# Layer 1's modulation written into PSUM banks, and two feature tiles of the first token half between the halves of V

## The chip, the cores and the metric

The kernel runs on one core of a Trainium2 chip. The time is the device time in microseconds (us) of one execution of the whole program. Beside the timed runs there is one profiled execution, whose trace the rows below come from.

TensorE is called PE in the profile (PEld is its weight load), VectorE is DVE, ScalarE is ACT, GpSimd is POOL, and SP issues DMAs.

## The reference, cut to what matters

Two layers of an encoder over 1024 tokens of width 1024. Each layer normalises its input, scales and shifts it by columns that depend on the conditioning vector (the modulation), projects it, attends, and adds the result back. The change lies at the seam: the end of layer 0, the modulation of layer 1 and the first projections of layer 1.

```python
h = rms_norm(x, norm_w[layer]) * (1.0 + scale[:, None, :]) + shift[:, None, :]
...
proj = h @ w_in
qc, kc, vc, gc = jnp.split(proj, [C_Q, C_Q + C_KV, C_Q + 2 * C_KV], axis=-1)
oc = windowed_sink_attention(qc.reshape(b, s, C_KV_HEADS, C_GROUPS, HEAD_DIM),
...
return (oc * jax.nn.silu(gc)) @ w_out
```

## The kernel before

Activations are kept transposed: 128 features on the partitions, tokens along the free dimension. The 1024 tokens are worked in two halves of 512, the 1024 features in eight tiles of 128 (KC = 8). Each float32 factor is split into a high part and a low remainder, so that one product costs three matmuls (mm3): high by high, high by low, low by high. So the modulated input of layer 1 exists as hT10h, hT10l (first token half) and hT11h, hT11l (second half).

No instruction is issued where it stands in the code. A Recorder collects every operation with its operands; `run` (line 249) lays them out in time by a list of cost estimates, and `emit` (line 477) issues them in that order, so that each engine executes a fixed order. Among the operations whose operands are ready and whose buffers are free, an engine takes the one with the lowest number: the number is the place in the program, plus a shift where one is given. FILL_SHIFT = 150 (line 44) puts the projections that fill gaps 150 places behind. PSUM has eight banks; PA (line 543) takes one, which comes free after the last operation on it. The estimate also keeps a VectorE instruction with two tensor inputs in SBUF and a GpSimd instruction from running at one time (`held`, line 450). All instructions are issued from line 483, so that every row says L483 and tells by its tile names what it is.

The stage that the change touches, in program order:

- layer0_out (line 1470), once for each token half: the output projection of layer 0 (eight feature tiles of 24 matmuls), the residual sum into `xr`, the sum of squares, and rstd_rows (line 678), which leaves the reciprocal norm of every token, spread over all partitions, in one PSUM bank. rows_copy (line 707) copies this bank to SBUF as `rby`. Then modulate (line 712) runs for each of the eight feature tiles: VectorE multiplies `xr` by the scale column and by `rby`, in place; ScalarE adds the shift and rounds to the high part h; VectorE adds the shift again and subtracts h, which gives the low part.
- V (line 1507): for each of eight token tiles of 128, 24 matmuls of 256 columns with the modulated input as weights, then a ScalarE and a VectorE instruction that bring the high and low part to SBUF. Tiles 0 to 3 need the first token half, 4 to 7 the second.
- Feature tiles of K, Q and the gate (fts, line 1663 on): each has two halves, one for each token half, of 24 matmuls of 512 columns. `fill` (line 1669) takes the next of them off the list `halves`, with the shift of 150. Six are placed ahead of the windowed attention: k0 for both halves, q0 for both, q1 for both. The weights of a tile are loaded by SP and split by GpSimd (high) and GpSimd again (low); wk1f0 is that of k0, wq1f0 that of q0.
- The windowed attention (win_S, win_PV), with the other 30 halves between its blocks.

A mark on a load, as marks["op", 0, 1, 6], makes the plan issue it no sooner than the start of that matmul (output projection of layer 0, second half, feature tile 6).

Of the kernel before, what the change touches and what calls it, by code (L numbers as in the profile page):

```python
# [14 lines left out]
ALU = mybir.AluOpType  # L15
# [7 lines left out]
NT = T // P  # L23
# [26 lines left out]
LAT_SHIFT = 100  # L50
FILL_J = (0,)
K2_POOL = 1
MOD_WAY = (("dve",), ("dve",))
E_START = (4, 4)
WARM = (32, 14, 20)
SQ_ENG = ("dve", "pool", "pool")
# [449 lines left out]
def encoder_kernel(ctx: ExitStack, tc: tile.TileContext, xt, ada_t, w_c1, w_c2, w_c3, w_g0, w_uq, w_ukv, w_out0, w_v1,  # L506
                   w_f1, w_out1, cols_d, rows_d, tabs_d, out, dump=None):
    if dump is None:
# [7 lines left out]
    psum = psp.tile([P, 4096], F32, name="psum")  # L516
# [7 lines left out]
    nc = rec = Recorder(tc.nc, tc, psum, {"u": U_BUFS, "ua": UA_BUFS, "sm": SM_BUFS}, window=WINDOW,  # L524
                        reserve=RESERVE)
    mm = nc.tensor.matmul

    def U(name, dt=F32):
        return rec.tile(up, [P, 1024], dt, name, "u")

    def UR(name):
        return U(name, F32R)
# [4 lines left out]
    def SM(name):  # L537
        return rec.tile(smp, [P, 16], F32, name, "sm")
# [4 lines left out]
    def PA(name):  # L543
        return rec.bank(1, name)
# [11 lines left out]
    @contextmanager  # L556
    def issue_after(mark):
        before = rec.after_now
        rec.after_now = mark if mark is not None else before
        yield  # L560
        rec.after_now = before
# [5 lines left out]
    def f(ap):  # L567
        return ap.bitcast(F32)
# [4 lines left out]
    def sub(o, a, b):  # L573
        nc.vector.tensor_tensor(out=o, in0=a, in1=b, op=ALU.subtract)
# [14 lines left out]
    def transposes(outs, ins, last):  # L589
# [3 lines left out]
        for j in order:  # L593
            with issue_after(m_):
                t_ = nc.tensor.transpose(out=outs(j), in_=ins[j], identity=ident)
            if last is not None:
# [11 lines left out]
                                   op0=ALU.add, op1=ALU.mult)  # L608
    cb = U("cb")
    for j in range(2):  # L610
        pt = PT(f"cb{j}")
        for k in range(4):
# [7 lines left out]
                                   op0=ALU.add, op1=ALU.mult)  # L620
# [5 lines left out]
    def warm(n, mark):  # L626
        pt = PT(f"warm{mark.i}")
        with rec.at(shift=5000), issue_after(mark):
            for _ in range(n):
                nc.tensor.transpose(out=pt[:, 0:P], in_=ident, identity=ident)  # L630
# [31 lines left out]
    def A_col(l, kc):  # L662
        return mods[:, 16 * l + 2 * kc:16 * l + 2 * kc + 1]

    def sh_col(l, kc):
        return mods[:, 16 * l + 2 * kc + 1:16 * l + 2 * kc + 2]


    def add_squares(acc, src, first, name, eng):

        if first:
            nc.scalar.activation(acc, src, AF.Square)
            return
        t = U(name)[:, 0:src.shape[1]]
        nc.scalar.activation(t, src, AF.Square)
        eng.tensor_tensor(out=acc, in0=acc, in1=t, op=ALU.add)

    def rstd_rows(accs, name):

        n = accs[0].shape[1]  # L680
        nt = n // P
        v = None
        for k, acc in enumerate(accs):
            pt = PA(f"st{name}")
            for j in range(nt):
                m_ = nc.tensor.transpose(out=pt[:, j * P:(j + 1) * P], in_=acc[:, j * P:(j + 1) * P], identity=ident)
            ss = SM("ss")
            nc.vector.tensor_reduce(out=ss[:, 0:nt], in_=pt[:, 0:n].rearrange("p (t c) -> p t c", t=nt), axis=AX.X,
                                    op=ALU.add)
            if k == 0:  # L690
                nc.vector.tensor_scalar(ss[:, 4:4 + nt], ss[:, 0:nt], 1.0 / D, EPS, op0=ALU.mult, op1=ALU.add)
            else:
                nc.vector.scalar_tensor_tensor(out=ss[:, 4:4 + nt], in0=ss[:, 0:nt], scalar=1.0 / D, in1=v, op0=ALU.mult,
                                               op1=ALU.add)
            v = ss[:, 4:4 + nt]
        if name == "x0" and WARM[1]:
            warm(WARM[1], m_)
        r = SM("r")
        nc.gpsimd.tensor_tensor(out=r[:, 0:nt], in0=v, in1=mhalf[:, 0:nt], op=ALU.pow)
        pr = PA(f"rb{name}")  # L700
        for j in range(nt):
            m_ = nc.tensor.transpose(out=pr[:, j * P:(j + 1) * P], in_=r[:, j:j + 1].broadcast_to([P, P]), identity=ident)
        if name == "x0" and WARM[2]:
            warm(WARM[2], m_)
        return pr[:, 0:n]

    def rows_copy(pr, name):
        rb = U(f"rb{name}")[:, 0:pr.proto().shape[1]]
        nc.scalar.copy(rb, pr)
        return rb  # L710

    def modulate(l, kc, src, rb, hl, way):

        h, lo = hl
        if way == "normed":
            nc.scalar.activation(h, src, AF.Identity, bias=sh_col(l, kc), scale=A_col(l, kc))
            nc.scalar.activation(src, src, AF.Identity, bias=sh_col(l, kc), scale=A_col(l, kc))
            sub(lo, src, f(h))
        elif way == "pool":
            nc.gpsimd.tensor_tensor(out=src, in0=src, in1=rb, op=ALU.mult)  # L720
            nc.scalar.activation(h, src, AF.Identity, bias=sh_col(l, kc), scale=A_col(l, kc))
            nc.gpsimd.tensor_scalar(src, src, A_col(l, kc), sh_col(l, kc), op0=ALU.mult, op1=ALU.add)
            sub(lo, src, f(h))
        else:
            nc.vector.scalar_tensor_tensor(out=src, in0=src, scalar=A_col(l, kc), in1=rb, op0=ALU.mult, op1=ALU.mult)
            nc.scalar.activation(h, src, AF.Identity, bias=sh_col(l, kc))
            nc.vector.scalar_tensor_tensor(out=lo, in0=src, scalar=sh_col(l, kc), in1=f(h), op0=ALU.add, op1=ALU.subtract)

# [27 lines left out]
    def hslice(hT, kc, i):  # L756
        h, l = hT[i // 4][kc]
        o = (i % 4) * P
        return h[:, o:o + P], l[:, o:o + P]
# [6 lines left out]
    def chunk(t, kc):  # L766
        return t[kc // 2][:, (kc % 2) * 512:(kc % 2 + 1) * 512]
# [27 lines left out]
    marks = {}  # L795
# [71 lines left out]
    for kc in range(KC):  # L867
        modulate(0, kc, chunk(xT[1], kc), rb0, hT0[1][kc], MOD_WAY[0][kc % len(MOD_WAY[0])])
    with issue_after(m_):
# [42 lines left out]
    for g in range(2):  # L912
# [9 lines left out]
        for b in range(2):  # L922
            for s in range(2):
                nc.vector.tensor_tensor(out=t2[:, :, b * 32 + s * 16:b * 32 + s * 16 + 16],
                                        in0=kr_[:, :, b * 32 + (1 - s) * 16:b * 32 + (1 - s) * 16 + 16],
                                        in1=ktab[1][:, :, b, s, :], op=ALU.mult)
# [120 lines left out]
    def ada_at(place, m0):  # L1047
        for n, a in enumerate(ada_place):
            if a == place:
                ada_fill(n, m0)  # L1050
# [419 lines left out]
    def layer0_out(half, oT, res, mark):  # L1470
        acc = U(f"sq1{half}")
        eng = nc.vector if SQ_ENG[1] == "dve" else nc.gpsimd

        def after(c0, n, ft):
            ada_at(("op", half, ft), marks["op", 0, half, ft])
            if ft % 2:
                nc.sync.dma_start(out=x1_sp[half, ft // 2], in_=res[ft // 2])
            if ft < 6:
                if ft % 2:
                    add_squares(acc, res[ft // 2], ft == 1, f"sq1{half}{ft}", eng)  # L1480
            else:
                if ft == 6:
                    eng.tensor_tensor(out=acc[:, 0:512], in0=acc[:, 0:512], in1=acc[:, 512:1024], op=ALU.add)
                add_squares(acc[:, 0:512], chunk(res, ft), False, f"sq1{half}{ft}", nc.vector)

        out_proj(0, wo0, oT, res, half, [(0, 512)], after, mark)
        rb = rows_copy(rstd_rows([acc[:, 0:512]], f"y{half}"), f"y{half}")
        hT1[half] = alloc_hT(1, half)
        for kc in range(KC):
            modulate(1, kc, chunk(res, kc), rb, hT1[half][kc], MOD_WAY[1][kc % len(MOD_WAY[1])])  # L1490

# [12 lines left out]

    wv1 = wload([w_v1[j] for j in range(2)], 256, "wv1", mark=marks["op", 0, 1, 3])
    V1 = [UR(f"V1{j}").rearrange("p (t g s d) -> p t g s d", t=2, g=4, s=2) for j in range(4)]
    for i in range(NT):
        ps = PA(f"v1_{i}")
        for kc in range(KC):
            mm3(ps[:, :256], hslice(hT1, kc, i), wv1[kc], kc == 0, kc == KC - 1)  # L1510
        v = ps[:, 0:256].rearrange("p (g d) -> p g d", g=4)
        vt = V1[i // 2][:, i % 2]
        nc.scalar.copy(vt[:, :, 0, :], v)
        sub(vt[:, :, 1, :], v, f(vt[:, :, 0, :]))
# [124 lines left out]
    def win_PV(g, i, Ps, lo, n, og):  # L1639
# [16 lines left out]
        for j in range(4):  # L1656
# [6 lines left out]
    fts = [("k", 0), ("q", 0), ("q", 1), ("q", 2), ("q", 3), ("g", 0), ("g", 1), ("q", 4), ("q", 5), ("k", 1),  # L1663
           ("g", 2), ("g", 3), ("q", 6), ("q", 7), ("g", 4), ("g", 5), ("G", 6), ("G", 7)]
    make = dict(k=k_ft, q=q_ft, g=g_ft, G=g_ft_late)
    fts = [make[a](p) for a, p in fts]
    halves = [(k, b) for k in range(len(fts)) for b in range(2)]

    def fill(mark):
        k, b = halves.pop(0)  # L1670
        with rec.at(shift=FILL_SHIFT):
            m_ = fts[k][1](b)
        if b == 0 and k + 1 < len(fts):
            fts[k + 1][0](m_)


    plan = [[0, 0, 0, 0, 1, 1, 1, 1], [1] * 8, [1] * 8, [1] * 8]
    fts[0][0](marks["op", 0, 1, 6])
    for _ in range(6):
        fill(None)  # L1680
    last = {}
    keep = {}
# [146 lines left out]
```

## Time and profile before

| | |
|---|---|
| median of 3 runs | 1215.26 us |
| the runs | 1213.6, 1215.26, 1216.71 us |
| the profiled execution | 1213.96 us, its span 1211.9 us |
| mean granted TensorE clock in it | 0.989 of 2.4 GHz |
| PE, DVE, ACT, POOL busy, share of the span | 97%, 77%, 54%, 46% |

The span runs from the first instruction to the last; all positions in rows are us from its start. 2.06 us of the profiled execution's time lie outside its span. A PE that is shown busy is not PE at its peak, as the ends of matmuls are modelled: the distance from the start of one matmul to the start of the next tells how fast it runs.

### The profile page before, as it was taken

The page shows a single profiled execution, that of the slowest core. Times are in us where ns is not written, and L with a number is a line of the kernel's source. Part 1 is how long each engine was busy: PE and PEld are TensorE (multiplying, and loading weights), DVE is VectorE, ACT ScalarE, POOL GpSimd, SP SyncE. Part 2 cuts the span into 40 slices and gives each one's busy share as a digit, 9 for nine tenths or more (in the row PEclk, how much of TensorE's full clock was granted, in tenths as well). Part 3 has the DMA queues.
Part 4 walks back from the last instruction along what each step waited for, and adds up shares of the span by engine and source line. Part 5 has one row for each costly group of instructions (what it writes and reads, how often), then busy time and mean ns, then how long its engine had stood idle before and what let it go on. Part 6 is the DMA issues. An engine that isn't in the chain of part 4 may idle for free.

```text
span 1211.9 us, 17927 instructions
## 1 busy us (share of the span) xinstructions
PE 1170.2 (97%) x6320; PEld 987.2 (81%) x6320; DVE 933.9 (77%) x1787; ACT 660.4 (54%) x1348; POOL 560.3 (46%) x551
## 2 busy tenths in 40 slices
PE   6999899999999999999999999899999999999996
PEld 5898778787878778778778888788888888888896
DVE  7976497888687988888789996839876598788343
ACT  4643356666555777787768122227765456653212
POOL 0057764435465555444448233504465265367321
PEclk9999899999999999999999999899999999999999
DMA  9601123131122220101034663100111121045112
GB/s 352 253 1 58 56 83 122 35 105 34 61 68 79 79 70 19 36 1 52 2 143 167 240 250 143 67 18 1 36 53 53 52 88 53 19 166 199 70 71 70
DMA packets 37338, 106.72 MB, mean 88 GB/s; under 512 B 3840, under 2 KB 9472, under 8 KB 37248
## 3 DMA queue, kind: packets, MB, share of 16 engines
q1 hardware_dynamic: 36480, 103.48, 23.7%
q0 software_dynamic: 768, 2.10, 0.7%
q8 instruction: 49, 0.80, 0.3%
q14 instruction: 41, 0.34, 0.1%
HBM read 82.36 MB, written 23.20 MB: 87 GB/s over the span
## 4 chain that ended last, share of the span: by engine, by line
PE 83%; DVE 10%; ACT 3%; issue 1%; DMA 1%; POOL 0%; SPq 0%; POOLq 0%; DVEq 0%; ACTq 0%
PE psum L483 83%; DVE nm L483 2%; DVE hla L483 1%; DVE p L483 1%; DVE hT11l L483 1%; DVE xr L483 1%; ACT q L483 1%; DVE Qa L483 1%; DMA xT<-in_xt 1%; ACT Pa L483 0%; DVE q L483 0%; ACT p L483 0%; DVE hl L483 0%; DVE hlb L483 0%; DVE ada L483 0%
## 5 line engine op out<-in xcount | busy, mean ns | idle before, releaser
L483 DVE TENSOR_REDUCE nm<-psum 128x1 f32<-128x1024 f32 x128 | 155.3, 1217 | 18.9 <-PE psum L483 17.2
L483 POOL TENSOR_SCALAR p<-p,dn 128x384 f32<-128x384 f32 (+1 forms) x128 | 74.1, 596 | 159.1 <-DVE dn L483 79.2
L483 DVE TENSOR_TENSOR hla<-psum,hla 128x512 fp32r<-128x512 f32 x128 | 84.9, 681 | 25.0 <-ACT hla L483 24.5
L483 PE MATMUL psum<-hla,VA 128*128 128x512 f32 x256 | 94.4, 421 | 5.4 <-DVE hla L483 4.0
L483 ACT CAST hla<-psum 128x512 fp32r<-128x512 f32 x128 | 72.5, 593 | 43.5 <-PE psum L483 37.2
L483 PE MATMUL psum<-ident,Pa 128*128 128x128 f32 x512 | 93.8, 272 | 0.8 <-DVE q L483 0.8
L483 POOL TENSOR_SCALAR Pb<-Pb,rs 128x1024 f32<-128x1024 f32 x64 | 71.8, 1124 | 45.6 <-DVE rs L483 43.9
L483 PE MATMUL psum<-hlb,VB 128*128 128x512 f32 x256 | 90.8, 427 | 2.2 <-DVE hlb L483 1.5
L483 POOL TENSOR_SCALAR Pa<-Pa,rs 128x1024 f32<-128x1024 f32 x64 | 76.4, 1198 | 34.8 <-DVE rs L483 32.1
L483 ACT ACTIVATE Pa<-psum,nm 128x1024 f32<-128x1024 f32 x64 | 71.6, 1120 | 32.0 <-DVE nm L483 24.7
L483 DVE TENSOR_TENSOR hlb<-psum,hlb 128x512 fp32r<-128x512 f32 x128 | 82.2, 683 | 7.7 <-ACT hlb L483 6.9
L483 ACT ACTIVATE Pb<-psum,nm 128x1024 f32<-128x1024 f32 x64 | 71.8, 1123 | 25.1 <-DVE nm L483 22.2
L483 PE MATMUL psum<-k,q 128*128 128x512 f32 x256 | 84.0, 399 | 0.2 <-ACT Pb L483 0.2
L483 PE MATMUL psum<-ident,Pb 128*128 128x128 f32 x512 | 79.4, 272 | 0.0
L483 DVE CUSTOM_DVE_ANT_0 p<-psum,bias,rows_g 128x384 f32<-128x384 f32 (+1 forms) x128 | 70.2, 577 | 10.7 <-PE psum L483 9.7
L483 ACT ACTIVATE p<-p,nm 128x384 f32<-128x384 f32 (+1 forms) x128 | 74.0, 585 | 7.1 <-DVE nm L483 7.1
L483 PEld LDWEIGHTS psum<-ident,Pa 128*128 128x128 f32 x512 | 65.0, 140 | 12.5 <-DVE q L483 1.0
L483 ACT CAST hlb<-psum 128x512 fp32r<-128x512 f32 x128 | 68.9, 603 | 9.1 <-PE psum L483 7.8
L483 ACT COPY ot<-psum 64x512 f32<-64x512 f32 x64 | 37.4, 584 | 65.7 <-PE psum L483 65.0
L483 PEld LDWEIGHTS psum<-ident,Pb 128*128 128x128 f32 x512 | 63.2, 140 | 11.2
L483 POOL TENSOR_TENSOR sq<-sq,sq 128x256 f32<-128x256 f32 (+2 forms) x22 | 26.9, 1222 | 79.9 <-ACT sq L483 79.7
L483 PE MATMUL psum<-oTl,wo1h 128*128 128x256 f32 (+1 forms) x192 | 61.1, 319 | 0.0
(749 smaller groups left out, 3672.3 us busy)
## 6 DMA issues: line engine op xcount, KB each, us to landing
ada<-in_ada_t SPq DMA_DIRECT2D x32, 512.0 KB, 8.2
adag<-in_ada_t SPq DMA_DIRECT2D x16, 512.0 KB, 4.8
o<-spill SPq DMA_DIRECT2D x12, 512.0 KB, 6.5
wo0s<-in_w_out SPq DMA_DIRECT2D x8, 512.0 KB, 8.4
xr<-in_xt SPq DMA_DIRECT2D x8, 512.0 KB, 9.6
x_sp<-xr SPq DMA_DIRECT2D x8, 512.0 KB, 3.0
wo1s<-in_w_out SPq DMA_DIRECT2D x8, 512.0 KB, 5.8
x1r<-x_sp SPq DMA_DIRECT2D x8, 512.0 KB, 5.3
```

The lines of the kernel that those rows point to most:

```text
L483: fn(*[real(v) for v in a], **{k: real(v) for k, v in kw.items()})
```

## The change

Four things change, all in layer 1's input:

- modulate gets a way "psum", which layer 1 uses for every feature tile of both halves (MOD_WAY). The scaled product is written to a PSUM bank of its own (`md`) and not back to `xr`; ScalarE and VectorE then read it there.
- The reciprocal norm is read by modulate from the PSUM bank in which rstd_rows leaves it; the copy to `rby` is gone.
- V is cut in two: token tiles 0 to 3, then two fills, then token tiles 4 to 7, then the other four fills.
- The list `halves` begins with k0 and q0 of the first token half, and then k0 and q0 of the second. The weights of k0 are marked by feature tile 4 of the output projection and not 6, and those of q0 by feature tile 6 and not by the first matmul of k0. The load of tile k + 1 is still tied to the first half of tile k from q0 on.

```diff
-MOD_WAY = (("dve",), ("dve",))
+MOD_WAY = (("dve",), ("psum",))
...
-            nc.vector.scalar_tensor_tensor(out=src, in0=src, scalar=A_col(l, kc), in1=rb, op0=ALU.mult, op1=ALU.mult)
+            if way == "psum":
+                t = PA(f"md{l}{kc}")
+                nc.vector.scalar_tensor_tensor(out=t, in0=src, scalar=A_col(l, kc), in1=rb, op0=ALU.mult, op1=ALU.mult)
+                src = t
+            else:
+                nc.vector.scalar_tensor_tensor(out=src, in0=src, scalar=A_col(l, kc), in1=rb, op0=ALU.mult,
+                                               op1=ALU.mult)
             nc.scalar.activation(h, src, AF.Identity, bias=sh_col(l, kc))
             nc.vector.scalar_tensor_tensor(out=lo, in0=src, scalar=sh_col(l, kc), in1=f(h), op0=ALU.add, op1=ALU.subtract)
...
-        rb = rows_copy(rstd_rows([acc[:, 0:512]], f"y{half}"), f"y{half}")
+        rb = rstd_rows([acc[:, 0:512]], f"y{half}")
...
-    for i in range(NT):
+
+    def v1_tile(i):
         ps = PA(f"v1_{i}")
...
-    halves = [(k, b) for k in range(len(fts)) for b in range(2)]
+    halves = [(0, 0), (1, 0), (0, 1), (1, 1)] + [(k, b) for k in range(2, len(fts)) for b in range(2)]
...
-        if b == 0 and k + 1 < len(fts):
+        if b == 0 and 0 < k < len(fts) - 1:
             fts[k + 1][0](m_)
...
-    fts[0][0](marks["op", 0, 1, 6])
-    for _ in range(6):
+    fts[0][0](marks["op", 0, 1, 4])
+    fts[1][0](marks["op", 0, 1, 6])
+    for i in range(4):
+        v1_tile(i)
+    for _ in range(2):
+        fill(None)
+    for i in range(4, NT):
+        v1_tile(i)
+    for _ in range(4):
         fill(None)
```

## Rows read from the trace of the kernel before

**Rows 1.** The page's first part (busy time, share, instructions of each engine) and the clock line of its second part (40 slices of the span, granted TensorE clock in tenths).

```profile
PE 1170.2 (97%) x6320; PEld 987.2 (81%) x6320; DVE 933.9 (77%) x1787; ACT 660.4 (54%) x1348; POOL 560.3 (46%) x551
...
PEclk9999899999999999999999999899999999999999
```

**Rows 2.** Busy time of each engine in chosen stretches: V of the first half, V of the second half, and what follows. Columns: stretch, its length, then each engine's busy us and instructions, granted clock, DMA share and rate.

```profile
754.38:766.85 12.47, 12.47 (x105) 12.38 (x104) 10.35 (x18) 4.01 (x8) 5.83 (x7) 1.00 0.48 170
766.85:787.39 20.54, 14.69 (x98) 13.48 (x97) 17.83 (x18) 5.08 (x10) 10.03 (x5) 0.83 0.00 1
787.39:798.30 10.91, 10.91 (x51) 9.02 (x49) 3.18 (x5) 2.69 (x5) 0.00 (x0) 1.00 0.00 1
798.30:820.00 21.70, 21.70 (x103) 18.35 (x102) 10.30 (x23) 5.87 (x10) 0.00 (x0) 1.00 0.08 25
```

**Rows 3.** The chain of work that ended last, around the second half's modulation: start, length, what.

```profile
762.42 0.59 ACT rby L483
...
763.04 3.27 DVE xr L483 x3
766.31 6.97 DVE hT11l L483 x3
773.28 2.77 DVE xr L483 x3
776.05 1.99 DVE hT11l L483 x3
778.03 3.48 DVE xr L483 x2
...
781.84 0.67 DVE hT11l L483
...
782.56 43.15 PE psum L483 x217
```

**Rows 4.** What PE's matmuls waited for between 754 and 790 us: total, times, longest.

```profile
PE psum L483 <- DVE hT11l L483: 5.7, 4, 1.9
```

**Rows 5.** PE's timeline, from V's first matmul to the second half of k0: start, duration, instruction, and idle time before it.

```profile
754.38 0.28 PE L483 MATMUL psum<-wv1h,hT10h 128*128 128x256 f32 x1
...
766.85 0.28 PE L483 MATMUL psum<-wv1h,hT11h 128*128 128x256 f32 x1
766.97 0.28 PE L483 MATMUL psum<-wv1l,hT11h 128*128 128x256 f32 x1
769.14 0.39 PE L483 MATMUL psum<-wv1h,hT11l 128*128 128x256 f32 x1 [1.89 <-DVE hT11l L483]
...
774.36 0.41 PE L483 MATMUL psum<-wv1h,hT11h 128*128 128x256 f32 x1
774.57 0.41 PE L483 MATMUL psum<-wv1l,hT11h 128*128 128x256 f32 x1
...
787.39 0.40 PE L483 MATMUL psum<-hT10h,wk1f0h 128*128 128x512 f32 x1
...
792.86 0.39 PE L483 MATMUL psum<-hT11h,wk1f0h 128*128 128x512 f32 x1
```

**Rows 6.** VectorE's timeline: an eviction of the output projection, and two groups of three low parts of the modulation.

```profile
749.14 0.75 DVE L483 SCALAR_TENSOR_TENSOR xr<-psum,gcol,xr 128x512 f32<-128x512 f32 x1 [4.69 <-PE psum L483]
...
766.23 7.05 DVE L483 SCALAR_TENSOR_TENSOR hT11l<-xr,mods,hT11h 128x512 fp32r<-128x512 f32 x3
...
775.97 2.06 DVE L483 SCALAR_TENSOR_TENSOR hT11l<-xr,mods,hT11h 128x512 fp32r<-128x512 f32 x3
```

**Rows 7.** GpSimd's timeline at the same places.

```profile
749.11 1.30 POOL L483 TENSOR_TENSOR sq<-sq 128x512 f32<-128x512 f32 x1
...
765.86 2.67 POOL L483 TENSOR_TENSOR wq1f0l<-wq1f0s,wq1f0h 128x1024 fp32r<-128x1024 f32 x1
768.51 1.48 POOL L483 TENSOR_SCALAR wq1f1h<-wq1f1s 128x1024 fp32r<-128x1024 f32 x1
770.07 2.66 POOL L483 TENSOR_TENSOR wq1f1l<-wq1f1s,wq1f1h 128x1024 fp32r<-128x1024 f32 x1
...
778.18 2.78 POOL L483 TENSOR_TENSOR wq1f2l<-wq1f2s,wq1f2h 128x1024 fp32r<-128x1024 f32 x1 [4.00 <-DVE hT11l L483]
```

**Rows 8.** Groups of instructions by shape, over the whole span (those of hT10, hT11 and V lie between 715 and 800 us): count, busy us, mean ns of one, idle time before them.

```profile
L483 DVE SCALAR_TENSOR_TENSOR gT<-gT,psum 128x512 f32<-128x512 f32 x16 | 10.9, 681 | 9.4 <-ACT gT L483 9.4
L483 DVE SCALAR_TENSOR_TENSOR hT10l<-xr,mods,hT10h 128x512 fp32r<-128x512 f32 x8 | 5.6, 740 | 0.0
L483 DVE TENSOR_TENSOR V<-psum,V 128x256 fp32r<-128x256 f32 x8 | 3.3, 418 | 4.0 <-ACT V L483 4.0
L483 ACT ACTIVATE hT11h<-xr,mods 128x512 fp32r<-128x512 f32 x8 | 5.7, 724 | 13.1 <-DVE xr L483 13.1
L483 ACT CAST hla<-psum 128x512 fp32r<-128x512 f32 x128 | 72.5, 593 | 43.5 <-PE psum L483 37.2 <-issue 3.8 <-POOL Pa L483 1.2
```

**Rows 9.** Busy time by stretches of the windowed attention (columns as in rows 2).

```profile
820.00:980.00 160.00, 159.03 (x833) 135.11 (x832) 124.34 (x376) 100.99 (x270) 78.81 (x104) 1.00 0.14 45
980.00:1140.00 160.00, 159.14 (x799) 133.51 (x799) 127.23 (x294) 83.03 (x209) 92.22 (x97) 1.00 0.29 104
```

**Rows 10.** SP's timeline: the issue of the weights of k0 and of q0.

```profile
733.97 0.42 SPq L483 DMA_DIRECT2D wk1f0s<-in_w_f  x1
...
756.79 0.42 SPq L483 DMA_DIRECT2D wq1f0s<-in_w_f  x1
```

## Prediction

> **What bounds the kernel now.** I read the page first: PE is busy for 97% of the span, the next engine for 77% [rows 1]. A kernel like this gets shorter only where PE stands still or runs slowly, so I looked for such a place near the change. The clock line has one dip in the middle, in its 26th slice [rows 1], and that slice (758 to 788 us) is where V's second half stands. Cut into stretches, the seam shows it [rows 2]: V of the first half fills its 12.47 us with PE busy throughout, V of the second half takes 20.54 us for fewer matmuls, with PE busy for 14.69 us and a mean granted clock of 0.83; what follows is full again. The chain that ended last leaves PE just there [rows 3]: from 762.42 to 782.56 it runs through ScalarE's copy `rby` and then through VectorE's modulation, tile after tile, and comes back to PE only with the last low part. PE's own waits name the same releaser, hT11l, four times [rows 4].
>
> How much is lost is read from the starts of matmuls [rows 5]. V's matmuls start 0.12 us apart (766.85, 766.97). The second half has 4 token tiles x 24 = 96 of them, 96 x 0.12 = 11.5 us of work; from its first matmul (766.85) to the first of k0 (787.39) it took 20.54 us. So **9.0 us** are lost. Most of that is standing still (5.7 us in the four named waits); the rest is matmuls at the lower clock after the first waits, 0.21 us apart (774.36, 774.57), which is the 1.2 GHz level, and shorter gaps.
>
> Why is the modulation slow? Its 16 VectorE instructions take 0.74 us each when alone [rows 8], and three in a row 2.06 us [rows 6], so that one follows another at (2.06 - 0.74) / 2 = 0.66 us. Sixteen at that pace are 10.6 us; the chain took 782.51 - 763.04 = 19.5 us [rows 3]. Three low parts took 7.05 us at 766.23 [rows 6], while GpSimd worked without a break on the weights of q0 and q1 [rows 7]: two tensor inputs in SBUF on VectorE, and GpSimd's work, exclude each other there. An instruction with one input in PSUM isn't held: the eviction at 749.14 took its usual 0.75 us [rows 6] beside GpSimd's sum of squares of 749.11 to 750.41 [rows 7].
>
> **The change part by part.** *The modulation in PSUM.* The 16 instructions of a half remain, but each now has one tensor input in SBUF and one in PSUM (`xr` and the norm; then `md` and h), so GpSimd no longer holds them. The ScalarE copy (0.59 us) goes from the head of the chain [rows 3]. Starting at 762.4, 16 x 0.66 = 10.6 us, plus four low parts of V in between (4 x 0.42 [rows 8] = 1.7), end at about 774.7 instead of 782.5. PE needs 12 matmuls for each feature tile (4 token tiles x 3), 1.44 us, VectorE supplies one in 2 x 0.66 = 1.33 us, and has a lead of 766.85 - 762.4 = 4.4 us. So V's second half would run through without a gap even with no fill behind it.
>
> No row shows VectorE writing to PSUM. Bounds for that one instruction: 0.68 us from below, as gT<-gT,psum, the same operation with one input in PSUM [rows 8]; from above 1.36, twice that, as if reading and writing PSUM took turns. I take 0.74, as its neighbours. At the upper end the chain is 8 x (1.36 + 0.66) + 1.7 = 17.9 us and ends at 780.3, and then the fill has to cover it, which it does (next part). ScalarE's h reads PSUM: between 0.59 (hla<-psum, without a bias) and 0.72 us, as now from SBUF [rows 8]; it isn't the slower of the two engines at either end.
>
> The eviction, which reads PSUM, takes 0.75 us [rows 6] and the low part with all operands in SBUF 0.74 [rows 8]: no fee for PSUM worth naming. The Trainium skill, Perfetto Trace Analysis, Optimizing Scalar/DVE Operations, speaks against this edit: it puts VectorE's access overhead at some 60 ns on SBUF and 125 ns on PSUM. By that (an estimate from that page) 16 instructions would cost 1.0 us more and VectorE's pace would fall to 1.46 us, just behind PE's 1.44; that would eat no more than 0.2 us of the lead and leave the sum, but it would make the first rival likelier.
>
> Banks: the norm holds one of eight until the eighth tile, `md` two or three, V's second half up to four. That leaves room for no or one fill, and `md` may have to wait for a bank; with two, a pair of tiles takes about 2 x 2 x 0.66 = 2.6 us plus hand-overs, which is PE's 2.9. In the first half the output projection holds one or two banks and PE doesn't need the result before V's first matmul at 754.38 [rows 5]. I cost both at nothing; if the cover by the fills were gone too, a chain with a single bank, each tile's three instructions in turn (0.74 + 0.72 + 0.74), would take 17.6 us and end near 780.
>
> *The two fills.* k0 and q0 of the first half are 24 matmuls each, (792.86 - 787.39) = 5.47 us [rows 5], 10.9 us together. Their input hT10 is ready: V's first matmul reads it at 754.38. The weights of k0 were issued at 733.97, those of q0 at 756.79 [rows 10]; by the new marks both go out earlier, k0's by up to two feature tiles of the output projection; SP's queue holds the stores of `xr` around them, which nobody waits for before the end of layer 1. GpSimd splits q0's in 1.5 + 2.7 us [rows 7], ahead of the pow instruction that opens the norm; if it came in its way, that costs up to 2.7 us of VectorE's lead, and the fill covers that. The fills have a higher number than V's tiles 4 to 6, so PE takes them only where V isn't ready. This is PE work moved, not added: with it PE has 766.85 + 11.5 + 10.9 = 789.3 us to reach the place that it reaches now at 787.39 + 10.9 = 798.3. Their evictions (4 and 2 instructions on each of ScalarE and VectorE) move along, into a stretch where VectorE has 20.5 - 17.8 [rows 2] + (19.5 - 10.6) = 11.6 us to spare once the holding is gone.
>
> *The sum.* 9.0 us of loss, of which I leave 0.4 us, a third of one of the present waits (5.7 / 4 = 1.4), since PE's order is fixed beforehand and some matmul may stand a little ahead of its operand: **-8.6 us**. Behind it PE is full: 159.0 and 159.1 of each 160 us [rows 9], with no wait on a load, so what is gained at 798 reaches the end. Profiled execution: 1213.96 - 8.6 = 1205.4. It lies 1.3 below the median of the runs, so the forecast for the median is 1215.26 - 8.6 = **1206.7 us**.
>
> **The rivals.** (1) *Half of it.* PE's order is fixed by estimates. If VectorE is slower than estimated, matmuls of V stand in front of the fills and wait. At the upper bound of the PSUM write, or with a single bank, the last low part comes at 780, and PE, with all of V ahead of the fills, wants it after seven of eight feature tiles, at 766.85 + 10.1 = 776.9: 3.4 us of wait, with as many shorter ones as now some 4.5, leave half the gain: about 1210.7. For: no row shows the write. Against: reading PSUM costs nothing extra, and the fills stand by.
> (2) *Not what it says.* The plan believes that V needs no filler and puts both fills behind it, and the modulation runs no faster since something other than GpSimd held it. Then nothing is gained: 1215. Against: the three low parts at 775.97, with GpSimd idle up to 778.18 [rows 7], took 2.06 us.
> (3) *More.* With q0 of the first half done by 778, the first scores and softmax of the window can start sooner on a VectorE that is busy for 10.3 of 21.7 us there [rows 2], and the seam to the windowed stage (PE loses 1.8 of 320 us there [rows 9]) tightens: at most 2 us more, 1204; beyond that there is nothing to gain.
> (4) *Slower.* The order of everything behind 754 is planned anew. VectorE is busy for 124 and 127 of 160 us in the windowed stage [rows 9], and a worse order there would make PE wait for its low parts. It decides from 9 + 3.7 us of new waits on; PE now loses those 1.8 us, so seven times that: 1219 is its price. Against: the list of fills and their number per block stay the same.
>
> **How the numbers follow.** About 0.3%, 3.65 us, is what a measurement of this kernel can tell from no change. Forecast (1205 to 1208.5) 0.64; (3) 0.10; (1) 0.14, of which a small part gains less than 3.65; (2) 0.07; (4) 0.05. Faster: 0.64 + 0.10 + 0.12 = 0.86; same 0.02 + 0.07 = 0.09; slower 0.05. The range takes in (3) and most of (1): 1203 to 1211.5; (2) and (4) stay outside.
>
> **What would show it.** V's second half without named waits of PE on hT11l, and the clock at 1.00 in that slice; three `md` products or low parts in a row at about 2.06 us while GpSimd works on weights; the last hT11l near 775; matmuls of k0 or q0 between V's; the first matmul of q1 some 9 us earlier. I am wrong if VectorE's write to PSUM takes over 1 us, if PE still waits for hT11l by over 2 us, or if PE's waits behind 820 grow by more than 2 us.

## The result, and the profile after

| | before | after |
|---|---|---|
| median | 1214.43 us (4 runs, 1212.39 to 1216.71) | 1205.54 us (4 runs, 1203.43 to 1206.6) |
| the profiled execution, its span | 1213.96, 1211.9 us | 1205.73, 1204.0 us |
| mean granted clock in it | 0.989 | 0.992 |

The ratio of the times is 0.9922, with a 95% interval of 0.9904 to 0.994: 8.9 us less between the medians, 8.2 between the profiled executions. The forecast was 8.6 less and a median of 1206.7.

The page after, the lines that answer to [rows 1]:

```profile
PE 1168.4 (97%) x6320; PEld 986.9 (82%) x6320; DVE 920.2 (76%) x1787; ACT 658.4 (55%) x1346; POOL 557.0 (46%) x551
...
PEclk9999899999999999999999999999999999999999
```

The dip of the clock in the 26th slice is gone. The same stretches as in [rows 2, 9], cut at V's first matmul, at the first of its second half and at the last of it:

```profile
755.32:767.69 12.37, 12.37 (x106) 12.37 (x104) 10.90 (x21) 3.52 (x7) 5.85 (x7) 1.00 0.38 128
767.69:782.58 14.89, 14.89 (x112) 14.20 (x111) 7.99 (x15) 4.43 (x9) 4.08 (x3) 1.00 0.11 36
...
820.00:980.00 160.00, 159.02 (x834) 134.85 (x833) 124.37 (x365) 100.17 (x262) 81.82 (x105) 1.00 0.15 50
980.00:1140.00 160.00, 159.15 (x792) 133.19 (x791) 120.42 (x272) 78.67 (x197) 89.46 (x93) 1.00 0.28 99
```

In V's second half PE is now busy for all of its 14.89 us, at clock 1.00, with 15 matmuls of k0 between V's 96. Both stretches of the windowed stage stand within 0.01 us of [rows 9]. The view of PE's waits has no row between 754 and 830 us, where it had four waits on hT11l, of 5.7 us [rows 4].

VectorE's timeline through the second half's modulation (start, duration, instruction, idle time before it), to be laid beside [rows 3, 6]:

```profile
763.22 2.07 DVE L483 SCALAR_TENSOR_TENSOR psum<-xr,mods,psum 128x512 f32<-128x512 f32 x3 [0.69 <-PE psum L483]
765.20 2.06 DVE L483 SCALAR_TENSOR_TENSOR hT11l<-psum,mods,hT11h 128x512 fp32r<-128x512 f32 x3
767.17 2.06 DVE L483 SCALAR_TENSOR_TENSOR psum<-xr,mods,psum 128x512 f32<-128x512 f32 x3
769.15 2.06 DVE L483 SCALAR_TENSOR_TENSOR hT11l<-psum,mods,hT11h 128x512 fp32r<-128x512 f32 x3
771.12 1.41 DVE L483 SCALAR_TENSOR_TENSOR psum<-xr,mods,psum 128x512 f32<-128x512 f32 x2
772.44 0.42 DVE L483 TENSOR_TENSOR V<-psum,V 128x256 fp32r<-128x256 f32 x1
772.77 1.40 DVE L483 SCALAR_TENSOR_TENSOR hT11l<-psum,mods,hT11h 128x512 fp32r<-128x512 f32 x2
```

GpSimd's, in the same time, beside [rows 7]:

```profile
764.80 1.05 POOL L483 TENSOR_SCALAR wq1f1h<-wq1f1s 128x1024 fp32r<-128x1024 f32 x1
765.93 2.41 POOL L483 TENSOR_TENSOR wq1f1l<-wq1f1s,wq1f1h 128x1024 fp32r<-128x1024 f32 x1
768.32 1.04 POOL L483 TENSOR_SCALAR wq1f2h<-wq1f2s 128x1024 fp32r<-128x1024 f32 x1
769.44 2.41 POOL L483 TENSOR_TENSOR wq1f2l<-wq1f2s,wq1f2h 128x1024 fp32r<-128x1024 f32 x1
```

Three instructions of VectorE in a row take 2.06 us with GpSimd at work beside them, as three did before only with GpSimd idle [rows 6, 7]. The chain, from the first product to the end of the last low part, runs from 763.22 to 772.77 + 1.40 = 774.17, 11.0 us. Before, it ran from 763.04 [rows 3] to the end of its last row on hT11l, with GpSimd at work (`bias`) from ahead of its start:

```profile
761.72 2.60 POOL L483 TENSOR_SCALAR bias<-relt 128x384 f32<-128x384 f32 x4
...
781.77 1.40 DVE L483 SCALAR_TENSOR_TENSOR hT11l<-xr,mods,hT11h 128x512 fp32r<-128x512 f32 x2
```

That is 783.17 - 763.04 = 20.1 us. GpSimd gains too: the low part of a weight tile takes 2.41 us and not 2.67 [rows 7].

PE's timeline, beside [rows 5]: the second half begins, k0's first matmul stands between V's, the first of q0, the first of q1:

```profile
767.69 0.28 PE L483 MATMUL psum<-wv1h,hT11h 128*128 128x256 f32 x1
...
777.39 0.40 PE L483 MATMUL psum<-hT10h,wk1f0h 128*128 128x512 f32 x1
777.63 0.28 PE L483 MATMUL psum<-wv1h,hT11h 128*128 128x256 f32 x1
...
784.76 0.39 PE L483 MATMUL psum<-hT10h,wq1f0h 128*128 128x512 f32 x1
...
802.29 0.39 PE L483 MATMUL psum<-hT10h,wq1f1h 128*128 128x512 f32 x1
```

And one piece of the chain that ended last, where [rows 3] had VectorE's pieces between 763 and 782:

```profile
699.88 116.45 PE psum L483 x619
```

**The measure used below** is the seam: from V's first matmul to the first matmul of q1. The same matmuls lie in it in every kernel here. Before it is 810.40 - 754.38 = 56.02 us, after 802.29 - 755.32 = 46.97: 9.05 less. The rest of the 8.23 between the profiled executions: V begins 0.94 later (what lies before it scatters; V begins between 753.77 and 758.93 in the kernels below whose layer 0 has the same source), what follows the seam takes 401.7 and not 401.5, and 0.3 less lies outside the span.

### The profile page after: what moved, and what is told of

Same layout as the page of the kernel before. It is cut to its first block, busy times and chain, and to the rows that moved or that the text cites. A ratio compares the mean times of both kernels' runs of the same rounds, so it can differ in the third digit from the quotient of the medians.

```text
span 1204.0 us, 17922 instructions
## 1 busy us (share of the span) xinstructions
PE 1168.4 (97%) x6320; PEld 986.9 (82%) x6320; DVE 920.2 (76%) x1787; ACT 658.4 (55%) x1346; POOL 557.0 (46%) x551
## 4 chain that ended last, share of the span: by engine, by line
PE 83%; DVE 9%; ACT 4%; issue 2%; DMA 1%; POOL 0%; SPq 0%; POOLq 0%; DVEq 0%; ACTq 0%
PE psum L483 83%; DVE nm L483 2%; DVE hla L483 1%; DVE p L483 1%; ACT q L483 1%; ACT k L483 1%; DVE Qa L483 1%; DMA ada<-in_ada_t 1%; ACT Pa L483 0%; DVE ada L483 0%; DVE q L483 0%; ACT p L483 0%; DVE hl L483 0%; ACT hlb L483 0%; DVE hlb L483 0%
## 5 line engine op out<-in xcount | busy, mean ns | idle before, releaser
L483 DVE TENSOR_REDUCE nm<-psum 128x1 f32<-128x1024 f32 x128 | 155.4, 1217 | 19.0 <-PE psum L483 17.4
```

Source lines behind the costliest of these rows:

```text
L483: fn(*[real(v) for v in a], **{k: real(v) for k, v in kw.items()})
```

## The experiments

Two theories stood at first. The one: GpSimd holds VectorE, PSUM frees it, and the whole gain is that. The rival: PE is kept busy by the two fills between V's halves. All runs in one table; the chain is the second half's modulation on VectorE, from its first product to the end of its last low part.

| run | chain, us | seam, us | median, us | ratio, 95% interval |
|---|---|---|---|---|
| before | 20.1 | 56.02 | 1214.43 | |
| after | 11.0 | 46.97 | 1205.54 | 0.9922 [0.9904, 0.994] |
| e1_psum_alone | 11.0 | 46.96 | 1205.43 | 0.9921 [0.9907, 0.9934] |
| e2_fills_alone | 17.2 | 53.13 | 1212.97 | 0.9976 [0.9966, 0.9985] |
| e3_norm_in_psum | 17.4 | 54.71 | 1213.48 | 0.9986 [0.9974, 0.9998] |
| e4_product_in_psum | 16.6 | 52.60 | 1213.07 | 0.9982 [0.9973, 0.9991] |
| e5_psum_alone_one_bank | 18.7 | 46.99 | 1205.92 | 0.9931 [0.9908, 0.9954] |
| e6_after_one_bank | 18.7 | 46.97 | 1207.03 | 0.9931 [0.9915, 0.9947] |
| e8_no_q_split | 12.1 | 47.34 | 1207.63 | 0.9936 [0.9917, 0.9956] |
| e9_fills_alone_ahead | 17.3 | 51.52 | 1209.79 | 0.9956 [0.994, 0.9973] |
| e10_estimate_only | 24.0 | 49.66 | 1207.49 | 0.9943 [0.9921, 0.9965] |
| e7_layer0_too | 11.0 | 46.97 | 1200.23 | 0.9888 [0.9869, 0.9907] |

The medians of the kernel before beside them were 1215.34 (e1 to e4; e5, e6, e8, e9) and 1214.28 (e7, e10).

**e1_psum_alone**: the PSUM half of the change on the kernel before; V, the fills, their order and their loads stay.

```diff
-MOD_WAY = (("dve",), ("dve",))
+MOD_WAY = (("dve",), ("psum",))
...
-        rb = rows_copy(rstd_rows([acc[:, 0:512]], f"y{half}"), f"y{half}")
+        rb = rstd_rows([acc[:, 0:512]], f"y{half}")
```

> The modulation in PSUM alone: V, the list of halves and the loads as before, no fill between V's halves. Measure beside the time: the seam, from V's first matmul to the first of q1, which was 56.0 us before and 47.0 after the change (same matmuls in it). Theory A (VectorE was held by GpSimd, and with one input in PSUM it isn't; the fills are cover that is not needed): the seam is 47 to 47.5 us, the last hT11l comes 10 to 11 us after the norm, the time is 8 to 9 us below before (ratio 0.9925 to 0.9935). Theory B (the fills close the gap, the faster modulation only helps): PE still waits 3 to 5 us on hT11l, the seam is 50 to 52 us, the time 4 to 5 us below before.

All of the gain is there: seam 46.96, 0.9921. VectorE beside GpSimd's splits of 1.06, 2.40, 1.05 and 2.40 us (768.22 to 775.3):

```profile
768.61 2.06 DVE L483 SCALAR_TENSOR_TENSOR hT11l<-psum,mods,hT11h 128x512 fp32r<-128x512 f32 x3
770.58 2.06 DVE L483 SCALAR_TENSOR_TENSOR psum<-xr,mods,psum 128x512 f32<-128x512 f32 x3
772.56 2.06 DVE L483 SCALAR_TENSOR_TENSOR hT11l<-psum,mods,hT11h 128x512 fp32r<-128x512 f32 x3
```

k0 starts at 782.63, right behind V's last matmul at 782.51, and PE has no wait: V's second half needs no fill.

**e2_fills_alone**: the other half of the change: after, with the modulation in SBUF and the copy of the norm.

```diff
-MOD_WAY = (("dve",), ("psum",))
+MOD_WAY = (("dve",), ("dve",))
...
-        rb = rstd_rows([acc[:, 0:512]], f"y{half}")
+        rb = rows_copy(rstd_rows([acc[:, 0:512]], f"y{half}"), f"y{half}")
```

> The split of V, the new order of the halves and the earlier loads alone: product in SBUF and the copy of the norm as before. Theory A with cover (10.9 us of ready matmuls are more than the 9.0 us of loss): the modulation still takes 17 to 20 us, but PE runs k0 and q0 between V's matmuls, seam 47 to 48 us, time 8 to 9 us below before. Rival: PE's fixed order comes from estimates that do not know how late VectorE is, so V's matmuls stand ahead of the fills and wait: seam 50 to 56 us, gain 0 to 5 us.

The fills alone bring 2.9 us of seam and not more. PE's waits, and two of VectorE's groups:

```profile
PE psum L483 <- DVE hT11l L483: 3.4, 3, 1.9
```

```profile
768.31 4.96 DVE L483 SCALAR_TENSOR_TENSOR hT11l<-xr,mods,hT11h 128x512 fp32r<-128x512 f32 x3
...
775.18 4.20 DVE L483 SCALAR_TENSOR_TENSOR hT11l<-xr,mods,hT11h 128x512 fp32r<-128x512 f32 x3
```

The low parts are held as before. k0's first matmul comes at 784.81, behind the waits: the plan took V to be ready and put the fill behind it, as rival (2) said. What is gained fits one weight split fewer beside the modulation: q0's is over by then, and the chain is 17.2 and not 20.1 us. I had expected the fill to cover, and it didn't.

**e8_no_q_split**: the kernel before, with q0, q1 and q2 using the weights of k0. It leaves out the loads and the splits of their own weights, so that GpSimd does no split during the modulation; two SBUF inputs remain.

```diff
+    w_k0 = []
...
+            if n in (2, 3, 4):
+                st["w"] = w_k0[0]
+                return
...
+            if n == 0:
+                w_k0.append(st["w"])
```

> The kernel before, but the weights of q0, q1 and q2 are neither loaded nor split: these three feature tiles use the weights of k0, so that six GpSimd instructions are missing beside the second half's modulation; VectorE's instructions are those of before, with two inputs in SBUF. Theory A (GpSimd's instructions hold VectorE): three low parts in a row take 2.06 us, only the four bias instructions still hold the first products by about 1.2 us, the chain takes 12 to 13 us instead of 19.5, seam 47 to 48.5 us, time 7.5 to 9 us below before. Rival (VectorE is slow there for another reason): the chain stays over 16 us and the seam over 52 us.

VectorE's timeline; GpSimd is busy with `bias` from 766.27 for 2.61 us and idle from there:

```profile
767.59 2.49 DVE L483 SCALAR_TENSOR_TENSOR xr<-xr,mods,rby 128x512 f32<-128x512 f32 x3 [1.41 <-ACT rby L483]
770.00 2.07 DVE L483 SCALAR_TENSOR_TENSOR hT11l<-xr,mods,hT11h 128x512 fp32r<-128x512 f32 x3
771.99 2.07 DVE L483 SCALAR_TENSOR_TENSOR xr<-xr,mods,rby 128x512 f32<-128x512 f32 x3
773.98 2.07 DVE L483 SCALAR_TENSOR_TENSOR hT11l<-xr,mods,hT11h 128x512 fp32r<-128x512 f32 x3
```

The same instructions that took 7.05 us in [rows 6] take 2.07. The chain is 12.1 us, PE has no wait, and the seam falls by 8.7. So it is GpSimd's work that made VectorE slow. The loads that e8 leaves out as well are no rival: in V's second half before, the DMA share is 0.00 [rows 2].

**e3_norm_in_psum** and **e4_product_in_psum** free one of the two kinds of instruction each, on the kernel before: in e3 the norm is read from PSUM and the product goes back to `xr`; in e4 the product goes to `md` and the norm is copied to SBUF.

```diff
 e3
-        rb = rows_copy(rstd_rows([acc[:, 0:512]], f"y{half}"), f"y{half}")
+        rb = rstd_rows([acc[:, 0:512]], f"y{half}")
 e4
-MOD_WAY = (("dve",), ("dve",))
+MOD_WAY = (("dve",), ("psum",))
```

> Without fills as before; only the norm is read from its PSUM bank (no copy), the product goes back to SBUF. So the 8 products have one input in SBUF, the 8 low parts still two. Theory A: the products follow one another at 0.66 us beside GpSimd's work, low parts are still held, by about the 5.0 us of before (7.05 + 2.06 + 1.40 against 16/2 at 0.66); seam about 51 to 52 us, gain 4 to 5 us. Rival (it was the copy and its hand-overs, or the place of the product, and not the holding): gain under 1 us, or all of 9.

> Without fills as before; the norm is copied to SBUF as before, only the product goes to PSUM. So the 8 products have two inputs in SBUF, the 8 low parts one. Theory A: low parts at 0.66 us beside GpSimd, products held by about the 4.1 us of before (3.27 + 2.84 + 3.55 against 8 at 0.66); seam about 51 to 52 us, gain 4 to 5 us. Rival (writing to PSUM is what slows or speeds VectorE): products at 1 us or more also where GpSimd is idle.

Both bring less than the 4 to 5 us that I had expected: 1.3 and 3.4 us of seam. In e3 the products run free and the low parts pay, in e4 the other way round. e3, VectorE:

```profile
761.77 2.06 DVE L483 SCALAR_TENSOR_TENSOR xr<-xr,mods,psum 128x512 f32<-128x512 f32 x3 [0.75 <-PE psum L483]
763.76 5.44 DVE L483 SCALAR_TENSOR_TENSOR hT11l<-xr,mods,hT11h 128x512 fp32r<-128x512 f32 x3
769.12 2.05 DVE L483 SCALAR_TENSOR_TENSOR xr<-xr,mods,psum 128x512 f32<-128x512 f32 x3
771.10 5.10 DVE L483 SCALAR_TENSOR_TENSOR hT11l<-xr,mods,hT11h 128x512 fp32r<-128x512 f32 x3
```

e4, VectorE:

```profile
767.38 2.06 DVE L483 SCALAR_TENSOR_TENSOR hT11l<-psum,mods,hT11h 128x512 fp32r<-128x512 f32 x3
769.35 5.11 DVE L483 SCALAR_TENSOR_TENSOR psum<-xr,mods,rby 128x512 f32<-128x512 f32 x3
774.38 2.06 DVE L483 SCALAR_TENSOR_TENSOR hT11l<-psum,mods,hT11h 128x512 fp32r<-128x512 f32 x3
```

GpSimd splits weights from 763.36 to 775.65 in e3 and from 765.43 to 777.80 in e4, with no gap over 0.1 us; one of its rows in e3:

```profile
768.74 2.70 POOL L483 TENSOR_TENSOR wq1f1l<-wq1f1s,wq1f1h 128x1024 fp32r<-128x1024 f32 x1
```

This sorts the kinds cleanly: beside it, three instructions with one SBUF input take 2.06 us and three with two 5.1 to 5.4 (3.3 in e4's first group, which begins before the splits do). It also suggests why half the cure isn't half the gain. GpSimd's queue of splits is the same, and what doesn't meet one VectorE group meets the next: before, three low parts took 7.05 and the next three 2.06 [rows 6]; in e3 it is 5.44 and 5.10. The chain shrinks by 2.7 and 3.6 us, together 6.3, where both at once bring 9.2.

**e5_psum_alone_one_bank** and **e6_after_one_bank**: e1 and after, with one `md` bank for each token half. It tests whether the change lives on spare banks.

```diff
+    md_of = {}
+
+    def md_bank(rb):
+        if rb.key not in md_of:
+            md_of[rb.key] = PA(f"md{rb.key}")
+        return md_of[rb.key]
...
-                t = PA(f"md{l}{kc}")
+                t = md_bank(rb)
```

> As the modulation in PSUM alone (no fill between V's halves), but all eight products of a half go to one and the same bank, so that a tile's product waits for the low part of the tile before. Both theories have VectorE free of GpSimd here. Expected: a tile takes product, high part and low part in turn, about 0.74 + 0.69 + 0.74 us and some 0.2 of hand-overs, 2.3 to 2.4 us, eight of them 18 to 19 us; PE runs out of V's matmuls, seam 54 to 56 us, nearly all of the gain gone (0 to 2 us below before). If banks did not matter: seam 47 us.

> The changed kernel with both fills, but with one bank for the products of a half. The modulation takes 18 to 19 us as in the run without fills; this time the plan knows of it, since the bank is part of its account. Theory (the fills cover a slow modulation if the plan has it in its account): k0 and q0 are issued between V's matmuls, PE does not wait on hT11l for more than 1 us, seam 47 to 48.5 us, 7 to 9 us below before. Rival (the fills stand behind V whatever the plan believes): seam 53 to 56 us.

e5, VectorE: product, wait for ScalarE's high part, low part, and only then the next product:

```profile
769.89 0.76 DVE L483 SCALAR_TENSOR_TENSOR psum<-xr,mods,psum 128x512 f32<-128x512 f32 x1
771.40 0.75 DVE L483 SCALAR_TENSOR_TENSOR hT11l<-psum,mods,hT11h 128x512 fp32r<-128x512 f32 x1 [0.76 <-ACT hT11h L483]
772.19 0.76 DVE L483 SCALAR_TENSOR_TENSOR psum<-xr,mods,psum 128x512 f32<-128x512 f32 x1
```

The chain takes 2.30 us for each tile and 18.7 in all, nearly as long as before. Yet PE has no wait, and the seam is 46.99. I had expected 54 to 56 for e5. The plan knows of the bank, so it knows that V will be late, and of its own accord it puts k0 between V's matmuls from 771.49 on, though V isn't split in e5. e6 does the same, with 16 matmuls of k0 between V's from 774.60 on; q0 comes behind V there, not between as I had expected, and PE has no wait. So this slow chain alone costs PE nothing. This changed the theory: the loss of before is the distance between the pace that the plan reckoned with and the real one.

**e10_estimate_only** tests that: the kernel before, the same instructions; only the plan's estimate of VectorE's scalar_tensor_tensor is 540 ns longer through the second half's modulation.

```diff
-            return 67 + 1.043 * m + 60 * npt + part, 0
+            return 67 + 1.043 * m + 60 * npt + part + (self.extra if method == "scalar_tensor_tensor" else 0), 0
...
+        rec.extra = 540 if half else 0
...
+        rec.extra = 0
```

> The kernel before with one thing changed, the plan's estimate: each VectorE instruction of the second half's modulation is entered 540 ns longer than before (1.20 us instead of 0.66), so that the plan's chain is as long as the measured one. What the engines execute is the same, in another order; PE's order now has k0's matmuls between V's. The run with one bank per half had shown fills between V's matmuls without any split of V, so the theory is now: the loss of before is the difference between the planned and the real pace of the modulation, and PE loses nothing if the plan knows the real pace. Expected by that: chain 18 to 20 us as before, PE waits under 1.5 us in all, seam 47 to 49 us, 7 to 9 us below before. Rival (only a faster modulation helps): seam over 53 us.

VectorE's chain is longer than ever, 24.0 us, and 6.4 of the 9.05 us come back. The rival is refuted, but my figures are all missed: chain 18 to 20, waits under 1.5, seam 47 to 49, and 6.8 us less and not 7 to 9. PE's waits:

```profile
PE psum L483 <- DVE hT11l L483: 1.7, 3, 0.8
```

k0 stands between V's matmuls from 771.89 on. Of the 2.7 us that it lacks against after, 1.7 are these waits, and most of the rest stands right beside them: measured from one matmul's start to the next, the three places lose some 2.5 us.

The plans themselves bear the theory out. In what `run` lays out, the second half's modulation takes 10.9 us in before, e1, e2, e3 and e4, and 18.5 in e5. The measured chains take 9.2, 0.1, 6.3, 6.5, 5.6 and 0.1 us more than that, and the seams lose 9.05, 0, 6.2, 7.7, 5.6 and 0 us against after; in e10 it is 24.0 us where the plan had 22.6, for a loss of 2.7. In the plan of before GpSimd does nothing while the modulation lasts, and the first split of q0's weights comes 26.9 us after V's first matmul. In the trace `bias` begins ahead of the first product and this split at 764.29, 9.9 us after V's first matmul. `held` parts the two engines in the plan alone; beyond operands and buffers, the order on each engine is all that the program hands over. No run keeps GpSimd back until the modulation is over.

**e9_fills_alone_ahead**: e2 with the first two fills at their place in the program, not 150 places behind it.

```diff
-    def fill(mark):
+    def fill(mark, shift=FILL_SHIFT):
...
-        with rec.at(shift=FILL_SHIFT):
+        with rec.at(shift=shift):
...
-        fill(None)
+        fill(None, 0)
```

> The fills alone (modulation as before, in SBUF), but the first two fills without the shift of 150, so that PE has k0 and q0 of the first half ahead of V's tiles 4 to 7. Theory (the fills alone failed only because they stood behind V in PE's fixed order): PE works through 10.9 us of fills while VectorE is held, V's second half then waits only where the chain's end at about 782 is late, seam 47.5 to 50 us, 6 to 8.5 us below before. Rival (it is not the order): seam above 52 us as in the run with the shift.

k0 and q0 now run from 768.6 to 779.7 and cover half: 4.5 us of seam, so that 51.52 lies between the 47.5 to 50 that I had expected and the rival's 52. Then PE meets another wait. Its timeline there:

```profile
782.56 0.36 PE L483 MATMUL psum<-wv1h,hT11h 128*128 128x256 f32 x1 [2.90 <-DVE V L483]
...
783.83 0.41 PE L483 MATMUL psum<-wv1h,hT11l 128*128 128x256 f32 x1
784.05 0.41 PE L483 MATMUL psum<-wv1h,hT11h 128*128 128x256 f32 x1
```

V's low part of a first-half tile stands on VectorE behind the held modulation (782.00, 0.41 us), and the matmul starts when it is done. Then about 15 matmuls run 0.21 us apart, at the lower clock, before 0.12 returns: 2.9 + 15 x 0.09 = 4.3, nearly all of the 4.55 us that are missing. Here the fill that is forced ahead has moved the wait to the next thing that VectorE owes.

**e7_layer0_too**: after, with the PSUM way in layer 0's second half also. Layer 0's modulation reads its norm from PSUM, too.

```diff
-MOD_WAY = (("dve",), ("psum",))
+MOD_WAY = (("psum",), ("psum",))
...
-    rb0 = rows_copy(xT_half(1), "x1")
+    rb0 = xT_half(1)
```

> The changed kernel with the modulation of layer 0's second token half done the same way (norm read in its bank, product in PSUM). PE had no standstill over 0.4 us between 30 and 130 us of the trace before, so no gain is expected: within 1.5 us of the changed kernel (1204 to 1207). If GpSimd's holding costs time there too, up to 3 us less.

I expected nothing, since PE has no wait in that stage, and 3 us less at most; it came out at 1200.23 us, 5.3 less than after and the best version here. In layer 0 the modulation's chain on VectorE falls from 17.3 us (70.19 to 87.53) to 11.6 (67.75 to 79.32). PE shows a gain only later. Windows of e7 and, below, of after:

```profile
120.00:140.00 20.00, 17.31 (x114) 15.41 (x113) 14.42 (x22) 8.09 (x15) 18.43 (x15) 0.91 0.16 52
140.00:160.00 20.00, 18.65 (x96) 15.14 (x94) 17.18 (x24) 9.46 (x16) 10.50 (x9) 1.00 0.46 145
160.00:180.00 20.00, 19.57 (x104) 15.51 (x102) 14.24 (x25) 13.44 (x24) 12.14 (x10) 1.00 0.01 1
```

```profile
120.00:140.00 20.00, 15.65 (x110) 14.07 (x109) 11.87 (x21) 8.31 (x16) 16.89 (x15) 0.92 0.16 54
140.00:160.00 20.00, 20.00 (x88) 16.21 (x87) 12.06 (x18) 7.09 (x12) 14.44 (x12) 0.91 0.22 71
160.00:180.00 20.00, 18.29 (x99) 14.19 (x99) 18.76 (x29) 10.01 (x19) 10.45 (x7) 1.00 0.23 88
```

PE stands for 4.5 us of these 60 and not 6.1, and one slice at 0.91 is at 1.00. Not all of the difference comes from there: V begins 6.0 us earlier than in after, and 1.8 of these are there at PE's matmuls on w13h (54.41 against 56.24), ahead of the modulation that was changed. Whether the earlier VectorE does this, or the new order that the plan finds behind it, no run here separates. It stays open.

## Why the prediction was right, step by step

**The loss of 9.0 us** was read rightly: the seam fell by 9.05. The 0.4 us that I left standing isn't there: PE has no wait in the seam, so this term of the sum was too large by the whole of itself. It is about the distance of the forecast (8.6) to the difference of the medians (8.9). The forecast of 1206.7 us itself is 1.2 too high; the other 0.8 is the median of before, which is 1214.43 with a fourth run and was 1215.26 with three.

**The chain of before** was read too short. The 19.5 us end with the last low part but one, after which PE goes on at 782.56 [rows 3]; the last one ends at 783.17, so the chain is 20.1. The 9.0 us of the sum don't rest on it.

**The cause, GpSimd holding VectorE**, is shown from both sides: take GpSimd's splits away and leave the SBUF inputs (e8: 2.07), or leave GpSimd and take one input to PSUM (e1: 2.06), and the holding is gone; leave both for one kind of instruction, and that kind pays (e3, e4). What the prediction gave only to its rivals is that the holding costs time because the plan doesn't have it: a chain of 18.7 us that the plan had cost nothing (e5). The Trainium skill, SBUF — State Buffer, Who interferes with whom, says the same: a VectorE instruction with two SBUF inputs contends with a GpSimd instruction that reads SBUF; one with at most one such input, outside VectorE's two-port performance modes, doesn't. The traces agree, with 5.1 to 5.4 us for three of the first kind and 2.06 for three of the second (e3, e4).

**The price of a PSUM write**, bounded by 0.68 and 1.36 us and taken as 0.74 with no row for it, is that of the neighbours. Groups of after, by shape, beside [rows 8]:

```profile
L483 DVE SCALAR_TENSOR_TENSOR psum<-xr,mods,psum 128x512 f32<-128x512 f32 x16 | 11.2, 749 | 0.7 <-PE psum L483 0.7
...
L483 DVE SCALAR_TENSOR_TENSOR hT10l<-psum,mods,hT10h 128x512 fp32r<-128x512 f32 x8 | 5.6, 742 | 0.0
...
L483 ACT ACTIVATE hT11h<-psum,mods 128x512 fp32r<-128x512 f32 x8 | 5.1, 693 | 3.9 <-DVE psum L483 3.9
```

742 stands against 740 ns with all operands in SBUF, and ScalarE's 693 against 724 [rows 8]. The Trainium skill's fee for PSUM (Perfetto Trace Analysis, Optimizing Scalar/DVE Operations: 125 ns for an access and 60 on SBUF) doesn't show here. The chain was put at 10.6 us and four low parts of V; it took 11.0, with one of these in it.

**"V's second half would run through without a gap even with no fill behind it"** is right: e1 does it.

**The fills** are where the reasoning fails though the sum doesn't. "The fill has to cover it, which it does" was to hold at the upper end of the PSUM price. e2 and e9 show that it doesn't if the plan doesn't see the delay: the fill stands behind the waiting matmuls (e2), or ahead, where it covers half and uncovers the next debt (e9). e5 and e6 show that it does when the plan sees it, with V whole and with V split, and e10 that it does for the greater part. The forecast was spared this by the low price of the write, which no row had shown; so far it was luck. In after the fills came at 777.39, when the chain had been over for three us, so they covered nothing; splitting V and moving the fills adds nothing that a measurement can tell (e1 against after: 0.9921 and 0.9922).

**Banks at nothing** was right, and for a better reason than I gave. With the cover gone I had a single-bank chain end near 780; its length was 18.7 and not 17.6 us, the hand-overs being most of the difference, and it cost no time, since the plan knew of the bank and put k0 between V's matmuls (e5, e6).

**The rivals.** (1) and (3) did not come: no wait is left, and the windowed stage runs as before [rows 9]. (2), that something other than GpSimd holds VectorE, is refuted by e8; its other half, that the plan puts the fills behind V, is what e2 shows. (4) did not come: 159.02 and 159.15 us.

## What to carry to other kernels

Where VectorE and GpSimd work side by side, count the SBUF tensor inputs of each VectorE instruction on the critical path, and bring every one of them down to one; half of them was worth less than half here (1.3 and 3.4 of 9 us). Where the order of an engine is fixed by estimates, a stage that is merely slow may cost nothing, and one that is slower than planned can cost the whole difference: compare the real pace of each feeding engine with the planned one before moving work about, and correct the estimate, which gave 6.4 of 9 us with no other change. In these runs a filler covered in full only a delay that the planner had been told of.

## What the runs showed of the hardware that I had not expected

- The holding goes both ways: GpSimd's low part of a weight tile (128x1024, two inputs) took 2.67 us beside a VectorE with two SBUF inputs [rows 7] and 2.41 beside one with a single one; its high part took 1.48 and 1.05 [rows 7, and after].
- The time that is lost to the holding isn't a property of an instruction: three low parts with two SBUF inputs took 2.06 or 7.05 us (before), 4.20 or 4.96 (e2), 5.10 or 5.44 (e3). In before the 2.06 fell where GpSimd was idle [rows 6, 7].
